# FFN layer two: the fifth outer product by seven inner products, inner weights made from the blocks in SBUF, and a first step emitted with high priority

## The chip, the cores and the metric

The kernel runs on one core of one Trainium2 chip. The metric is the device time of one execution in microseconds (us). The core has five engines with an instruction queue each: PE (TensorE, matmuls, with its weight loads shown apart as PEld), DVE (VectorE), ACT (ScalarE), POOL (GpSimd) and SP (SyncE, which here only issues DMAs). An engine takes its instructions in order, so an instruction that waits holds up all that stand behind it on that engine.

## The reference, cut to what matters

```python
def reference(x, ...):                       # x: 1 x 2048 x 1024, float32
    ...                                      # token mixers, output projection -> h
    hn2 = rmsnorm(h, norm2_g)
    up = jnp.einsum('bsd,df->bsf', hn2, w_up)        # 2048 x 1024 @ 1024 x 4096
    act = jnp.square(jax.nn.relu(up))
    h = h + jnp.einsum('bsf,fd->bsd', act, w_down)   # 2048 x 4096 @ 4096 x 1024
    return rmsnorm(h, final_g)
```

The change concerns the product `act @ w_down`, called layer two here.

## The kernel before

All activations are held transposed, features on the 128 partitions and 512 tokens along the row. A float32 operand of a matmul is split into a high part `hi` (ACT, L146) and a rest `lo` (DVE, L147), and a product is three matmuls: weight hi by row hi, weight hi by row lo, weight lo by row hi. Each matmul is 128x128 by 128x512.

**Outer products.** Both feed-forward layers go by the Winograd form of Strassen's scheme: the weights are four blocks, the tokens two halves (`PAIRS`, two times 512 tokens each), the features two halves, and seven products P1 to P7 of sums of blocks take the place of eight. In layer two (`down`) the row operands are the seven sums A11, A12, A22, S1, S2, S3, S4 of activations, which layer one (`up`) leaves in DRAM as `sd[q][i]`, with q the half of the product's columns. A plain outer product is 8 steps, one for each 256 features (`kk`), and a step is 2 values of q x 4 blocks of 128 output features x 2 chunks of 128 features x 3 matmuls, 48 matmuls, 384 in the eight (L1390).

**Inner products.** P4 and P2 (`SPLIT`) are themselves made by the same scheme, of seven inner products on blocks of a quarter of the size: 28 steps of 12 matmuls, 336 (L1228). They need sums of quarter blocks of the weights (`wi`) and of the rows (`sdi`). The sums of rows are made in `up` as the activations come out (`inner_rows` loads the other half's rows, `inner_sums` makes four sums and stores them, L870 and L879 to L887). The sums of weights are made in `down`, in the steps of the outer product ahead (`inner_weights`, `prepare`): quarter blocks are loaded again from DRAM (L1088, rows of 1 KB), subtracted in place (L1096) and stored (L1097). The order is P1, P6, P7, P4, P5, P2, P3.

**Weights of the outer products.** `make` builds a step's operands: `blk` loads a block of weights of 512 KB (L1121), `minus` makes a difference of two blocks in place (L1125) and can store it as `td[0]` or `td[1]` (L1127) for a later product; two row tiles `ar` are loaded (L1171) and split into `ad`, the weights into `wd`. P1 loads b11, and for `td[0]` also b12; P6 takes `td[0]`, b22 and b21 and leaves `td[1]`; P7 takes b12 and b22; P5 takes `td[0]` again.

**What runs ahead.** `make_ahead` emits operands of steps until six row operands and three weight operands are ahead of the matmuls. The buffers are five of `ar`, six of `wr`/`wq` (loaded weights), three of `wd` and five of `ad`. All these pools of `down` lie in memory that `up` used, so their first tiles wait until `up` has let go of it.

**Results.** `evac` and `inner_step` take the sums in PSUM (tile `pb`, eight banks) into the tiles p1, u2, u3, c21; a POOL-issued DMA adds the residual h to them (`add_residual`); `final` makes the sums of squares for the last norm, on ACT and DVE. P5 as a plain product ends with 16 additions on DVE, onto u3 and u2. The last outer product, P3, runs for one q after the other, with the last norm of finished parts between its steps and the rest behind it.

**What sets the order.** The program is written as a plain sequence; a scheduler then places the instructions of all engines by their dependences and by its own estimates of durations, so the order on each engine isn't that of the text. `tc.high_priority()` puts what is emitted in it ahead of other work that is ready. At the boundary between the layers the operands of the first steps of `down` are therefore loaded and split among the last activations of `up` (`post`, L976 to L1025).

Of the kernel before, what the change touches and what calls it, by code (L numbers as in the profile page):

```python
# [46 lines left out]
def hymba_block(ctx: ExitStack, tc: tile.TileContext, xT, gains, w_in, pool_w, w_out, w_up, w_down, out):  # L47
# [64 lines left out]
    for i in range(PAD):  # L112
# [24 lines left out]
    sdi = {i: [[dram.tile([P, 2, T], F32, name=f"sdi{i}_{n}_{c}") for c in range(4)] for n in range(4)] for i in (1, 2)}  # L137
    wi = {i: {n: [dram.tile([P, 4, 256], F32, name=f"wi{i}_{n}_{c}") for c in range(2)]
              for n in ("P5", "P6", "P7", "P4")} for i in (1, 2)}
    td = [[dram.tile([P, 2, T], F32, name=f"td{i}_{c}") for c in range(8)] for i in range(2)]  # L140
# [717 lines left out]
    def up(pools, more):  # L858
# [110 lines left out]
        def post(q, m, s):  # L969
# [4 lines left out]
            def put(i, t):  # L974
                if q == 0 or m >= NM // 2 or i not in (A12, A22):
                    nc.sync.dma_start(sd[q][i][m // 2][:, m % 2], t)  # L976
                if q and i in (A12, A22):
                    inner_sums(m, i, t)
# [23 lines left out]
            elif s == "P7":  # L1002
                copy("u3")
# [64 lines left out]
    def down(pools):  # L1068
        t8, s8, rs, rt, pupa, pup, rsp, rlp, tmp_, psb = pools

        SPLIT = {"P4": A22, "P2": A12}
        order = (("P1", A11), ("P6", S2), ("P7", S3), ("P4", A22), ("P5", S1), ("P2", A12))
        steps = []
        for n, i in order:
            if n in SPLIT:
                steps += [(n, p, kk, None) for p in ("P1", "P5", "P6", "P3", "P7", "P2", "P4") for kk in range(4)]
            else:
                steps += [(n, i, kk, (0, 1)) for kk in range(8)]
        steps += [("P3", S4, kk, (q,)) for q in range(2) for kk in range(8)]
        made = {}  # L1080

        def quarter(of, kp, x, y):
            t = rt.tile([P, 4, 256], F32, tag="wr", name="wq")
            v = t.rearrange("p (k c) n -> p k c n", k=2)
            for k in range(2):
                at = 2 * kp + k + 4 * x
                src = w_down[of, at] if isinstance(of, int) else td[int(of[1]) - 1][at]
                nc.sync.dma_start(v[:, k], src[:, :, y * 256:(y + 1) * 256])  # L1088
            return t

        def inner_weights(n):

            i, res = SPLIT[n], []

            def less(to, x, y, p, kp):
                nc.vector.tensor_tensor(to, x, y, ALU.subtract)  # L1096
                nc.sync.dma_start(wi[i][p][kp], to)  # L1097

            for kp in range(2):
                b = {}  # L1100

                def take(x, y, b=b, kp=kp):
                    return lambda: b.update({(x, y): quarter(source[n], kp, x, y)}), lambda: None
                op = lambda to, x, y, p, b=b, kp=kp: (lambda: None, lambda: less(b[to], b[x], b[y], p, kp))
                res += [take(0, 0), take(0, 1), op((0, 0), (0, 1), (0, 0), "P5"), take(1, 1),
                        op((0, 1), (1, 1), (0, 1), "P7"), op((1, 1), (1, 1), (0, 0), "P6"), take(1, 0),
                        op((1, 0), (1, 0), (1, 1), "P4")]
            return res

        prep, source = [], {"P4": "t2", "P2": 2}  # L1110

        def prepare(n):

# [460 lines left out]
```

## Time and profile before

| what | value |
|---|---|
| runs: median, lowest to highest of three | 1929.7 us, 1928.63 to 1931.03 us |
| the profiled execution: its own time, its span | 1929.1 us, 1927.3 us |
| busy: DVE, ACT, POOL | 1365.9 us, 990.4 us, 177.3 us |
| layer one, `up` (matmuls L1052) | about 695 to 1308.8 us of the span |
| layer two: P1, P6, P7 | 1313.5 to 1576.9 us |
| P4 (inner) | 1576.9 to 1653.1 us |
| P5 | 1653.1 to 1740.1 us |
| P2 (inner) | 1740.1 to 1816.3 us |
| P3 and the last norm | 1816.3 us to the end |
| DMA traffic | 483.44 MB, mean 251 GB/s |

How to read it: a line of groups has the line of the kernel, the engine, the operation, the tiles written and read, their shapes, the count, then the busy time in us and the mean time of one in ns. Durations of successive instructions on an engine can overlap by some 0.1 us; the distance between starts is the cost in the queue. A stretch of the trace ("windows") gives its length, then for each engine the busy time and the instructions in brackets, then the clock that TensorE was granted (1.00 is full speed), the share of time in which the DMA engines were busy and their rate in GB/s. A list of instructions gives start, duration, engine, line, operation, tiles, count, and in brackets the idle time ahead of it with what ended it.

### The profile page before, as it was taken

The numbers are of one execution on the slowest core, as the hardware profiler recorded it, in microseconds if no ns is written. First come the engines' busy times: TensorE is split into PE (matmuls) and PEld (weight loads), VectorE is DVE, ScalarE is ACT, GpSimd is POOL, SyncE is SP. The second block draws the span as 40 slices with busy tenths as digits, with TensorE's granted clock in tenths as the row PEclk, the third lists the DMA queues.
The fourth block names the chain that finished last, engine by engine and source line by source line (L and its number), as shares of the span: only waits on it lengthen the run. The fifth ranks groups of instructions, "written<-read, shape, count | busy, mean of one in ns | idle before, by whom it ended". The sixth has DMA issues, their size and how long they took to land.

```text
span 1927.3 us, 26270 instructions
## 1 busy us (share of the span) xinstructions
PE 1903.3 (99%) x9043; PEld 1588.9 (82%) x9043; DVE 1365.9 (71%) x2026; ACT 990.4 (51%) x1580; POOL 177.3 (9%) x399
## 2 busy tenths in 40 slices
PE   9999999999999999999999999998999999999997
PEld 7888888888888888888888888887888888888886
DVE  6887799667866976667678767776555547648874
ACT  5565566455554455555576555553333255426643
POOL 0211123101211120000000000000010010002120
PEclk9999999999999999999999999999999999999999
DMA  7685686887797864676667566669798888959852
GB/s 224 206 273 179 222 277 212 262 310 262 263 344 277 304 204 150 211 248 228 212 230 253 195 219 221 243 248 396 268 326 291 276 251 312 333 192 303 312 207 90
DMA packets 197359, 483.44 MB, mean 251 GB/s; under 512 B 22496, under 2 KB 42976, under 8 KB 193120
## 3 DMA queue, kind: packets, MB, share of 16 engines
q1 hardware_dynamic: 192464, 473.01, 70.9%
q0 software_dynamic: 4608, 8.39, 2.4%
q8 instruction: 73, 1.20, 0.3%
q14 instruction: 70, 0.57, 0.1%
q10 hardware_dynamic: 144, 0.26, 0.1%
HBM read 320.10 MB, written 161.48 MB: 250 GB/s over the span
## 4 chain that ended last, share of the span: by engine, by line
PE 92%; DVE 4%; DMA 2%; issue 1%; POOL 1%; ACT 1%; SPq 0%; DVEq 0%; ACTq 0%; POOLq 0%
PE pb L1390 22%; PE pY L1052 17%; PE pZ L1052 9%; PE pb L1228 8%; PE pd L175 8%; PE pd L176 8%; PE pd L177 8%; PE pX L1052 4%; PE po L672 2%; PE pta L661 1%; PE pm L202 1%; PE pz L614 1%; PE pr L228 1%; PE pz L615 1%; PE pb L1333 1%
## 5 line engine op out<-in xcount | busy, mean ns | idle before, releaser
L1390 PE MATMUL pb<-ad,wd 128*128 128x512 f32 x1872 | 429.4, 391 | 4.7 <-ACT ad L146 4.7
L1390 PEld LDWEIGHTS pb<-ad,wd 128*128 128x128 f32 x1872 | 352.3, 189 | 78.1 <-ACT ad L146 5.1
L1052 PE MATMUL pY<-sa,hw 128*128 128x512 f32 x1536 | 364.1, 389 | 0.7 <-ACT u L987 0.7
L1052 PEld LDWEIGHTS pY<-sa,hw 128*128 128x128 f32 x1536 | 288.1, 188 | 60.9 <-ACT u L987 1.1
L175 PE MATMUL pd<-h,hl 128*128 128x512 f32 x752 | 300.0, 399 | 0.7 <-DVE qkr L421 0.7
L176 PE MATMUL pd<-h,hl 128*128 128x512 f32 x752 | 297.4, 395 | 0.0
L177 PE MATMUL pd<-h,hl 128*128 128x512 f32 x752 | 297.2, 395 | 0.0
L146 ACT ACTIVATE ad<-ar 128x1024 fp32r<-128x1024 f32 x136 | 142.4, 1052 | 116.2 <-PE pb L1390 69.9
L147 DVE TENSOR_TENSOR ad<-ar,ad 128x1024 fp32r<-128x1024 f32 x136 | 164.8, 1222 | 39.6 <-ACT ad L146 39.5
L1052 PE MATMUL pZ<-sa,hw 128*128 128x512 f32 x768 | 184.6, 389 | 0.0
L1052 PEld LDWEIGHTS pZ<-sa,hw 128*128 128x128 f32 x768 | 144.1, 188 | 29.9
L175 PEld LDWEIGHTS pd<-h,hl 128*128 128x128 f32 x752 | 142.3, 189 | 28.4 <-DVE qkr L421 1.0
L177 PEld LDWEIGHTS pd<-h,hl 128*128 128x128 f32 x752 | 142.2, 189 | 27.9
L176 PEld LDWEIGHTS pd<-h,hl 128*128 128x128 f32 x752 | 142.1, 189 | 27.1
L146 ACT ACTIVATE hl<-raw 128x512 fp32r<-128x512 f32 x168 | 104.2, 631 | 111.0 <-PE pd L177 67.2
L1228 PE MATMUL pb<-ad,wd 128*128 128x512 f32 x672 | 152.7, 389 | 0.0
L147 DVE TENSOR_TENSOR hl<-raw,hl 128x512 fp32r<-128x512 f32 x168 | 114.3, 687 | 53.6 <-ACT hl L146 50.0
L1228 PEld LDWEIGHTS pb<-ad,wd 128*128 128x128 f32 x672 | 126.1, 188 | 26.2
L146 ACT ACTIVATE wd<-wr 128x1024 fp32r<-128x1024 f32 x48 | 50.9, 1062 | 151.2 <-PE pb L1390 129.5
L147 DVE TENSOR_TENSOR hw<-rt,hw 128x512 fp32r<-128x512 f32 x128 | 87.6, 688 | 57.3 <-ACT hw L146 56.5
L147 DVE TENSOR_TENSOR wd<-wr,wd 128x1024 fp32r<-128x1024 f32 x48 | 58.6, 1223 | 62.0 <-ACT wd L146 62.0
L1052 PE MATMUL pX<-sa,hw 128*128 128x512 f32 x384 | 93.1, 389 | 0.0
(213 smaller groups left out, 2591.6 us busy)
## 6 DMA issues: line engine op xcount, KB each, us to landing
ar<-sd SPq DMA_DIRECT2D x104, 512.0 KB, 5.7
rb<-in_w_up_dram SPq DMA_DIRECT2D x32, 1024.0 KB, 5.8
wr<-in_w_down_dram SPq DMA_DIRECT2D x64, 512.0 KB, 5.5
sd<-a SPq DMA_DIRECT2D x112, 256.0 KB, 3.2
raw<-in_w_in_dram SPq DMA_DIRECT2D x50, 512.0 KB, 4.3
sd<-s SPq DMA_DIRECT2D x96, 256.0 KB, 3.5
raw<-in_w_out_dram SPq DMA_DIRECT2D x32, 512.0 KB, 5.5
ar<-sdi SPq DMA_DIRECT2D x32, 512.0 KB, 7.2
```

The costliest lines, as they stand in the source:

```text
L146: nc.scalar.activation(hi, src, AF.Copy)
L147: return nc.vector.tensor_tensor(lo, src, hi.bitcast(F32), ALU.subtract)
L175: nc.tensor.matmul(ps, hl[:, 0, c], hi, start=(k == 0), stop=False)
L176: nc.tensor.matmul(ps, hl[:, 0, c], lo, start=False, stop=False)
L177: mm = nc.tensor.matmul(ps, hl[:, 1, c], hi, start=False, stop=(k == n - 1))
L202: marks["pm"] = nc.tensor.matmul(pm[:, c:c + 1], ss[:, c * P:(c + 1) * P], inv[n], start=(i == 0), stop=(i == len(parts) - 1))
L228: mm = nc.tensor.matmul(pr[:, b * P:(b + 1) * P], yr[:, x, b:b + 1].to_broadcast([P, P]), identr, start=(b == 0 and x == 0), stop=(b == TB ...
L614: nc.tensor.matmul(pz, qa[:, qsl], k, start=first, stop=False, skip_group_check=not (first and last))
L672: nc.tensor.matmul(po[:, p * 256 + to:p * 256 + to + hi - lo], vw[:, 2 * p + v], at[:, x, lo:hi], start=(p == 0 and n == 0 and x == 0), sk ...
L1052: nc.tensor.matmul(t, w[:, wx, c], a[:, ax, c % 2], start=first and c == 0 and x == 0, stop=last and c == G - 1 and x == 2, skip_group_che ...
L1228: nc.tensor.matmul(b, t[:, wx, 2 * (kk % 2) + c, i * P:(i + 1) * P], a[:, ax, c], start=p in ("P1", "P5", "P2") and kk == 0 and c == 0 and ...
L1390: nc.tensor.matmul(ps[q, n], t[:, wx, c, n * P:(n + 1) * P], left_[q][:, ax, c], start=(n_ in ("P1", "P5", "P3") and kk == 0 and c == 0 an ...
```

## The change

1. **P5 joins P4 and P2.** It is made by seven inner products (`SPLIT` gets P5, with the rows S1). Its 16 additions at the end become 28, four behind each inner product, on u3 and on u2, and the residuals are added as a part is complete.
2. **`up` makes the inner sums of S1** as well as of A12 and A22: for each of the eight pairs of columns with q = 1 two more loads of rows, four more operations on DVE, four more stores, and one store of S1 less.
3. **Inner weights from blocks in SBUF.** `quarter` loads for the sums, `prepare` and its list go. A block's last use in a step is now to be turned into the inner differences in place (`more_weights`, `inner_weights`: four subtractions of 128x512 and four stores of 256 KB for each pair of blocks kk, kk + 4). To have both in SBUF, the steps of P1, P6 and P7 run in the order 0, 4, 1, 5, 2, 6, 3, 7 (`TURN`). P1 makes those of `td[0]` (for P5), P6 those of `td[1]` (for P4), P7 loads b12 once more and makes those for P2. The order inside a weight block is changed on the host, so that a half of its columns lies in one piece (`half`, `block`).
4. **P6's b21 gets a buffer of its own**, `rtx`, one tile. Half of `td[1]` is stored for kk below 4.
5. **The first step of P1 is emitted with high priority**, without its differences, which follow (`late`).

The diff, cut:

```diff
-    sdi = {i: [[dram.tile([P, 2, T], F32, name=f"sdi{i}_{n}_{c}") for c in range(4)] for n in range(4)] for i in (1, 2)}
+    sdi = {i: [[dram.tile([P, 2, T], F32, name=f"sdi{i}_{n}_{c}") for c in range(4)] for n in range(4)] for i in (1, 2, 3)}
...
             def put(i, t):
-                if q == 0 or m >= NM // 2 or i not in (A12, A22):
+                if q == 0 or m >= NM // 2 or i not in (A12, A22, S1):
                     nc.sync.dma_start(sd[q][i][m // 2][:, m % 2], t)
-                if q and i in (A12, A22):
+                if q and i in (A12, A22, S1):
                     inner_sums(m, i, t)
...
             elif s == "P7":
+                if q and m >= NM // 2:
+                    inner_rows(m - NM // 2, S1)
                 copy("u3")
...
-        SPLIT = {"P4": A22, "P2": A12}
+        SPLIT = {"P4": A22, "P5": S1, "P2": A12}
+        TURN = (0, 4, 1, 5, 2, 6, 3, 7)
...
-                steps += [(n, i, kk, (0, 1)) for kk in range(8)]
+                steps += [(n, i, kk, (0, 1)) for kk in TURN]
...
+        def inner_weights(i, kk, t):
+            if kk < 4:
+                tops[i] = t
+                return
+            b, k = {(x, y): half(w, y) for x, w in enumerate((tops.pop(i), t)) for y in range(2)}, kk - 4
+            for to, x, y, p in (((0, 0), (0, 1), (0, 0), "P5"), ((0, 1), (1, 1), (0, 1), "P7"),
+                                ((1, 1), (1, 1), (0, 0), "P6"), ((1, 0), (1, 0), (1, 1), "P4")):
+                nc.vector.tensor_tensor(b[to], b[x], b[y], ALU.subtract)
+                nc.sync.dma_start(wi[i][p][k // 2][:, 2 * (k % 2):2 * (k % 2) + 2], b[to])
...
+        def more_weights(n, kk, w):
+            if n == "P1":
+                minus(blk(1, kk), w)
+                nc.sync.dma_start(td[0][kk], w)
+                inner_weights(S1, kk, w)
+            elif n == "P6":
+                minus(blk(2, kk, rtx), w)
+                if kk < 4:
+                    nc.sync.dma_start(half(td[1][kk], 0), half(w, 0))
+                else:
+                    nc.sync.dma_start(td[1][kk], w)
+                inner_weights(A22, kk, w)
+            elif n == "P7":
+                inner_weights(A12, kk, blk(2, kk))
...
+            late.append(lambda: more_weights(n, kk, w))
+            if g:
+                late.pop()()
...
-            elif n_ == "P5":
-                add(val("u3", q), val("u3", q))
-                add_residual(val("u3", q)[:, n], j1, 1, n)
-                add(val("u2", q), val("u2", q))
-                add_residual(val("u2", q)[:, n], j0, 1, n)
...
+                    for name in {"P4": ("c21",), "P5": ("u3", "u2"), "P2": ("p1",)}[n_]:
+                        to = val(name, q)[:, n]
+                        nc.vector.tensor_tensor(to, b, to, ALU.add)
...
+                        elif n_ == "P5":
+                            add_residual(to, PAIRS[q][name == "u3"], 1, n)
...
+        with tc.high_priority():
+            make_ahead(1)
+        late.pop()()
         make_ahead()
         for g, (n_, i, kk, qs_) in enumerate(steps):
-            if n_ in ("P7", "P5") and kk == 0:
-                prep.extend(inner_weights("P4" if n_ == "P7" else "P2"))
-                prep[0][0](), prep[1][0]()
-            if n_ in ("P7", "P5"):
-                prepare(2)
```

The scheduler places other rows too. Three places show it, all at the boundary between the layers, where the last activations of `up` and the first operands of `down` share DVE and ACT. L881 to L887 are the inner sums of rows; L1012 to L1021 before, L1014 to L1023 now, are the last sums and the last activation of `up` (the row that reads `pZ` is the one behind the very last matmuls of `up`); L1125 before and L1115 now is `minus`; L1106 is a subtraction of `inner_weights`.

DVE before, from the third weight operand of `down` to the first row operands:

```order
L147 TENSOR_TENSOR wd<-wr,wd 128x1024
L881 TENSOR_TENSOR j_13261<-a_13105,a_13256 128x512
L1125 TENSOR_TENSOR wr<-wr 128x1024
L883 TENSOR_TENSOR j_13262<-j_13261,hr 128x512
L885 TENSOR_TENSOR hr<-hr,a_13105 128x512
L887 TENSOR_TENSOR hr<-hr,j_13262 128x512
L1012 TENSOR_TENSOR s_13286<-a_13283,a_13256 128x512
L1015 TENSOR_TENSOR s_13289<-s_13286,a_13204 128x512
L1017 TENSOR_TENSOR a_13283<-a_13204,a_13283 128x512
L1021 TENSOR_TENSOR a_13306<-pZ,u_13224 128x512
L147 TENSOR_TENSOR ad<-ar,ad 128x1024 x5
```

Between the third `minus` and the row that reads `pZ` stand six rows, and the row operands `ad` follow that row.

DVE now, from the same place, first part:

```order
L147 TENSOR_TENSOR wd<-wr,wd 128x1024
L881 TENSOR_TENSOR j_13379<-a_13220,a_13374 128x512
L1115 TENSOR_TENSOR wr<-wr 128x1024
L883 TENSOR_TENSOR j_13380<-j_13379,hr 128x512
L885 TENSOR_TENSOR hr<-hr,a_13220 128x512
L887 TENSOR_TENSOR hr<-hr,j_13380 128x512
L1106 TENSOR_TENSOR wr<-wr 128x512 x4
```

and on to the first row operands:

```order
L1014 TENSOR_TENSOR s_13404<-a_13401,a_13374 128x512
L881 TENSOR_TENSOR j_13407<-s_13269,s_13404 128x512
L1019 TENSOR_TENSOR a_13401<-a_13318,a_13401 128x512
L1106 TENSOR_TENSOR wr<-wr 128x512
L883 TENSOR_TENSOR j_13408<-j_13407,hr 128x512
L1017 TENSOR_TENSOR s_13417<-s_13404,a_13318 128x512
L885 TENSOR_TENSOR hr<-hr,s_13269 128x512
L887 TENSOR_TENSOR hr<-hr,j_13408 128x512
L1023 TENSOR_TENSOR a_13434<-pZ,u_13338 128x512
L147 TENSOR_TENSOR ad<-ar,ad 128x1024 x5
```

The four subtractions of `inner_weights` and a fifth one, and the four inner sums of S1, now stand between `minus` and the row that reads `pZ`: fifteen instructions where there were six. The first `ad` still follows that row.

ACT before, the last activations of `up` and the first rows of `down` (L981 and L982 are relu and square):

```order
L981 ACTIVATE a_13204<-a_13204 128x512
L982 ACTIVATE a_13204<-a_13204 128x512
L987 ACTIVATE u_13254<-pY 128x512
L146 ACTIVATE wd<-wr 128x1024
L981 ACTIVATE a_13256<-a_13256 128x512
L982 ACTIVATE a_13256<-a_13256 128x512
L981 ACTIVATE a_13283<-pY 128x512
L982 ACTIVATE a_13283<-a_13283 128x512
L981 ACTIVATE a_13306<-a_13306 128x512
L146 ACTIVATE ad<-ar 128x1024 x5
```

and ACT now:

```order
L987 ACTIVATE u_13372<-pY 128x512
L981 ACTIVATE a_13318<-a_13318 128x512
L982 ACTIVATE a_13318<-a_13318 128x512
L146 ACTIVATE wd<-wr 128x1024
L981 ACTIVATE a_13374<-a_13374 128x512
L982 ACTIVATE a_13374<-a_13374 128x512
L981 ACTIVATE a_13401<-pY 128x512
L982 ACTIVATE a_13401<-a_13401 128x512
L146 ACTIVATE ad<-ar 128x1024 x2
L981 ACTIVATE a_13434<-a_13434 128x512
L146 ACTIVATE ad<-ar 128x1024 x3
```

The first two row operands `ad` have moved ahead of the relu on the last activation; the rest still follows it. Before, a pair L981, L982 on an earlier activation stood ahead of the copy L987, and the third weight operand `wd` followed the copy directly; now that pair stands between the copy and the weight operand.

101 lines of the change are left out of this document (39 added, 62 removed).

## The prediction

> **What bounds the kernel now.** I read the page first, then the waits of PE, then the chain of work that ended last.
>
> ```profile
> span 1927.3 us, 26270 instructions
> PE 1903.3 (99%) x9043; PEld 1588.9 (82%) x9043; DVE 1365.9 (71%) x2026; ACT 990.4 (51%) x1580; POOL 177.3 (9%) x399
> ```
> ```profile
> PE pb L1390 <- ACT ad L146: 4.7, 1, 4.7
> PE pzero L327 <- DVE zero L95: 1.5, 1, 1.5
> ```
> ```profile
> 1313.51 263.43 PE pb L1390 x1152
> 1576.94 76.16 PE pb L1228 x336
> 1653.10 87.04 PE pb L1390 x384
> 1740.14 76.17 PE pb L1228 x336
> ```
>
> PE is busy for all but 24 us of the span. It waits for operands once for long: 4.7 us, at the boundary between the layers. Inside layer two it runs without a stop: 336 matmuls take 76.16 us and 384 take 87.04 us, 226.7 ns each in both forms. So a change pays here if it takes matmuls away or closes that gap, and costs where it makes PE wait.
>
> The gap has a tail. These stretches run across it; the last but two column is the granted clock:
>
> ```profile
> 1308.00:1310.00 2.00, 0.82 (x4) 0.36 (x2) 1.94 (x4) 0.43 (x1) 0.00 (x0) 1.00 1.06 414
> 1310.00:1313.50 3.50, 0.00 (x0) 0.00 (x0) 1.86 (x4) 1.62 (x3) 0.00 (x0) 0.65 1.01 412
> 1313.50:1316.00 2.50, 2.49 (x6) 2.01 (x7) 2.50 (x3) 2.50 (x3) 0.00 (x0) 0.50 1.06 419
> 1316.00:1318.00 2.00, 2.00 (x7) 1.55 (x6) 2.00 (x2) 1.77 (x3) 0.00 (x0) 0.53 1.01 405
> 1318.00:1320.00 2.00, 2.00 (x11) 1.64 (x10) 1.97 (x4) 0.00 (x0) 0.00 (x0) 1.00 1.05 405
> ```
>
> In the gap the clock falls, stays at half until about 1318, and PE then does 13 matmuls in 4.5 us. The 1152 matmuls take 263.43 us where 1152 x 0.2267 is 261.1: this tail costs 2.3 us. The boundary costs 7.0 us in all.
>
> **The change part by part.** *P5.* 384 matmuls become 336: 87.04 - 76.16 = 10.9 us off PE. This is the one gain that needs nothing else.
>
> *The boundary.* What holds PE there is DVE. These are its rows from the trace, the third weight operand to the first rows of `down`:
>
> ```profile
> 1304.38 1.23 DVE L147 TENSOR_TENSOR wd<-wr,wd 128x1024 fp32r<-128x1024 f32 x1 [0.34 <-ACT wd L146]
> 1305.56 0.69 DVE L881 TENSOR_TENSOR j<-a,a 128x512 f32<-128x512 f32 x1
> 1306.17 1.22 DVE L1125 TENSOR_TENSOR wr<-wr 128x1024 f32<-128x1024 f32 x1
> 1307.30 0.68 DVE L883 TENSOR_TENSOR j<-j,hr 128x512 f32<-128x512 f32 x1
> ...
> 1311.16 0.69 DVE L1021 TENSOR_TENSOR a<-pZ,u 128x512 f32<-128x512 f32 x1
> 1313.49 5.77 DVE L147 TENSOR_TENSOR ad<-ar,ad 128x1024 fp32r<-128x1024 f32 x5 [1.64 <-ACT ad L146]
> ```
> ```profile
> 1305.94 2.88 PE L1052 MATMUL pZ<-sa,hw 128*128 128x512 f32 x12
> 1302.44 0.60 ACT L987 ACTIVATE u<-pY 128x512 f32<-128x512 f32 x1 [1.53 <-PE pY L1052]
> 1303.28 1.07 ACT L146 ACTIVATE wd<-wr 128x1024 fp32r<-128x1024 f32 x1 [0.24 <-DMA wr<-in_w_down_dram]
> 1304.24 0.62 ACT L981 ACTIVATE a<-a 128x512 f32<-128x512 f32 x1
> 1304.89 0.63 ACT L982 ACTIVATE a<-a 128x512 f32<-128x512 f32 x1
> 1307.80 0.64 ACT L982 ACTIVATE a<-a 128x512 f32<-128x512 f32 x1
> ```
>
> PE ends `up` at 1305.94 + 2.88 = 1308.8. The row L1021, which reads its last result, starts only at 1311.16: from 1306.17 on DVE runs without idling, a `minus`, six rows of 128x512 at a distance of 0.64 us (3.86 / 6), then L1021. It is late, not waiting. The order above shows nine more rows of that size in this place: five subtractions of inner weights and four inner sums of S1. DVE pays 9 x 0.64 = 5.8 us more before it is through with the row that reads `pZ`. That row releases the second row operand on ACT, and behind it on DVE stand all `lo` parts of the rows. The high priority has moved the first `hi` part ahead, so PE can do the four products hi by hi of q = 0 early, 0.9 us, and then waits on.
>
> In numbers: `minus` is also later, since L981 and L982 on an earlier activation now stand between the copy L987 and the weight operand on ACT, 2 x 0.65 less the 0.24 idle, so it starts at about 1307.3. Then 1.13 + 15 x 0.64 + 0.69 ends the `pZ` row at 1318.8; the second `hi` takes 1.1 us more on ACT; PE goes on at 1319.9. Idle: 1319.9 - 1308.8 - 0.9 = 10.2 us, for 4.7 before, + 5.5 us. The half clock behind it stays, 2.3 us in both.
>
> The subtractions work in place, so they also wait until the block's store has landed:
>
> ```profile
> wr<-in_w_down_dram SPq DMA_DIRECT2D x11, 512.0 KB, 8.1
> td<-wr SPq DMA_DIRECT2D x3, 512.0 KB, 6.8
> ```
>
> A store takes 6.8 us around the boundary. That of the third `minus` is issued at about 1308.5 and lands at 1315.3; by its own queue DVE reaches the subtraction behind it at 1308.4 + 10 x 0.64 = 1314.8. So + 0.5 us: the boundary costs 6.0 us more than before. Its ends: 4.4 us if neither the ACT order nor a store delays anything, 10 us if stores land as late as the slowest 11.1 us load there, `wr` in this row of the chain:
>
> ```profile
> 1292.18 11.07 DMA wr<-in_w_down_dram
> ```
>
> The Trainium skill, "DMA: Bandwidth & Descriptors", section "Anatomy of one DMA", fits a DMA by 2.0 us and bytes at 436 GB/s, which is an estimate of 3.2 us for 512 KB. By that no store would be in the way and the sum would be 0.5 us lower; the measured 6.8 us speaks against it here, where the queue is full.
>
> *More sums in `up`.* 32 more operations on DVE, 32 x 0.64 = 20.5 us, and 10.5 MB more traffic (8 pairs of columns x 5 x 256 KB) in this stretch:
>
> ```profile
> 1005.00:1309.00 304.00, 303.14 (x1337) 250.35 (x1335) 226.00 (x352) 170.81 (x297) 0.00 (x0) 1.00 0.66 235
> 1309.00:1402.00 93.00, 88.49 (x381) 73.10 (x382) 50.42 (x48) 32.05 (x36) 5.44 (x6) 0.96 0.88 319
> 1402.00:1490.00 88.00, 88.00 (x390) 72.86 (x389) 45.71 (x40) 29.13 (x34) 1.74 (x2) 1.00 0.93 317
> 1653.00:1740.00 87.00, 87.00 (x386) 72.03 (x385) 44.79 (x45) 25.71 (x26) 6.44 (x8) 1.00 0.75 252
> 1740.00:1816.00 76.00, 76.00 (x337) 62.91 (x336) 66.82 (x73) 48.62 (x55) 7.60 (x9) 1.00 1.02 331
> ```
>
> DVE goes from 226 to some 247 of 304 us and DMA from 0.66 to some 0.75: hidden by PE's 303. I take 0; without that cover it would be 2.6 us for each of the eight pairs.
>
> *P1 and P6 (rows two and three).* Counted from the program in blocks of 512 KB, P1 moved 40 (two weights, two rows and a store in each of eight steps), and the stores of inner weights make it 48; P6 moved 48, now 54. Shares of 0.88 and 0.93 become about 1.05 in both, 4 to 5 us too much in each stage. DVE gets 16 subtractions in each, 10 us, and waits for stores, and in P6 for the one buffer of b21. The cover is the lead of the operands:
>
> ```profile
> 1338.71 1.23 DVE L147 TENSOR_TENSOR wd<-wr,wd 128x1024 fp32r<-128x1024 f32 x1 [4.21 <-ACT wd L146]
> ```
> ```profile
> DVE wr L1125 <- DMA wr<-in_w_down_dram: 31.3, 7, 6.4
> ```
>
> This weight operand is made as the second step ends (1313.51 + 2.3 + 2 x 10.88 = 1337.6) and needed two steps of 10.9 us later, at 1359.3: 19 us of lead. In P6 DVE already waits 31.3 us for weights, up to 6.4 us at once, and PE never stops. I take 0 and keep + 13 us as the other end (third rival).
>
> *P5's own work.* DVE has 42 splits of 1.15 us (5.77 / 5) and 28 additions of 0.64, 66 us of 76; P2's stage has 66.82 of 76 (row five) without a stop. The residuals fall in its second half instead of at its end. I take 0; the other end is the second rival.
>
> *Sum.* - 10.9 + 6.0 = - 4.9 us, 1924.2 us by the profiled execution's own 1929.1. The median of the runs shown lies 0.6 us above that, so **1924.8 us**.
>
> **The rivals.** *First: the gap closes.* If the first step runs as the priority asks, PE stops for some 0.7 us (ACT is through with the last L982 at 1308.4, the split takes 1.05), and neither the 4.7 us nor the 2.3 us are paid: 1929.7 - 10.9 - 6.3 = 1912.5 us. ACT's order speaks for it, DVE's fifteen rows ahead of the first `lo` against it. By the Trainium skill, "TensorE: Matmul & The Clock Gate", section "What's actually happening", the clock halves after about 3.4 us of idling; the rows agree with that (4.7 us, then 0.50), and a gap of 0.7 us would keep it whole.
>
> *Second: P5 waits for its own sums.* ACT squares u3 for the last norm as soon as its residuals have landed, ahead of splits for P2:
>
> ```profile
> ACT sq L1247 <- DMA u<-hs: 9.6, 4, 4.3
> u<-hs POOLq DMA_DIRECT2D x9, 256.0 KB, 14.2
> ```
>
> The longest of these waits was 4.3 us and hidden. Residuals now follow the inner products one by one, and inner steps have a lead of four steps of 2.7 us, 10.9. If a 14.2 us landing isn't covered, some 5 us are lost: 1929.8 us.
>
> *Third, the other side: P6 runs DVE late.* A pair of steps has 6 splits, 4 `minus` and 4 subtractions, 6.9 + 4.5 + 2.6 = 14.0 us, of 21.8. Two waits of 4 us for stores and two of 2.5 us for b21, both inside the 6.4 us of the row above, make it 27, 5.2 us too long, 21 us over the four pairs. It decides as soon as this is more than the lead that is left. With the 19 us whole it costs next to nothing; if the late start at the boundary and P1's full DMA leave 8 us, PE loses 13: 1938 us. For it: shares above 1, in-place work behind stores. Against it: P6's 42 us in which DVE is idle now.
>
> **How the numbers follow.** Forecast 0.62, its own range 1923 to 1929 by the boundary's two ends; first rival 0.09, second 0.12, third 0.17. A measurement here can tell about 0.2% from no change, so faster is below 1925.8 and slower above 1933.6. The forecast falls below 1925.8 as long as the boundary costs under 7.0 us more, some three quarters of its chance: 0.47; with the first rival 0.56. The rest of the forecast and most of the second rival make no change, 0.26; the third, and a little of the second, make slower, 0.18. The range that leaves out the first rival and most of the third is 1916 to 1934 us.
>
> **What would show it.** Right: 336 matmuls in 76.2 us for P5; PE idle for 9 to 11 us at the boundary in two pieces with four matmuls between them, the longer one ending with the first rows' split, half clock behind it; no wait of PE in P1, P6 and P7; DMA shares near 1 in P1 and P6. Wrong: a boundary of under 3 us (first rival), waits of PE for `wd` or `ad` in P6 (third) or at the start of P2 (second), or stops in the second half of `up`, where I counted nothing.

## The result and the profile after

| | median, lowest to highest | runs |
|---|---|---|
| before | 1929.56 us, 1927.54 to 1933.19 | 7 |
| changed | 1937.83 us, 1933.86 to 1939.64 | 7 |

The ratio is 1.0043, with a 95% interval of 1.0033 to 1.0053: the change makes the kernel 8.3 us slower, where 4.9 us faster were forecast, and the time lies outside the forecast's range of 1916 to 1934 us. The profiled execution took 1938.5 us.

The head of the page, then all waits of PE above 1.7 us:

```profile
span 1936.7 us, 26464 instructions
PE 1895.5 (98%) x8995; PEld 1581.6 (82%) x8995; DVE 1425.2 (74%) x2120; ACT 1008.5 (52%) x1598; POOL 177.2 (9%) x399
```
```profile
PE pb L1392 <- ACT ad L146: 16.2, 2, 9.8
PE pY L1054 <- ACT u L987: 4.4, 2, 3.1
PE pm L202 <- DVE ss L186: 2.7, 1, 2.7
```

The span is 9.4 us longer. PE works 7.8 us less than before and waits more: 16.2 us for the first row operands, where it was 4.7. The chain of work that ended last (start, us, what) says where the ground is lost:

```profile
1297.82 7.91 DMA wr<-in_w_down_dram
1305.75 8.89 DMA wr<-in_w_down_dram
1315.94 7.62 DMA td<-wr
1333.58 263.10 PE pb L1392 x1148
1596.68 168.65 PE pb L1221 x744
1771.16 54.47 PE pb L1221 x239
1825.64 5.45 PE pb L1392 x24
```

P7 ends at 1596.7, before at 1576.9: 19.7 us later. The three inner products end at 1825.6, 229.0 us behind it, where P4, P5 and P2 took 239.4: 10.4 us regained. And the chain ahead of P1 is now made of DMAs, two weight loads and the store of a difference. PE's rows across the boundary (start, us, operation, count, and in brackets the idle time ahead):

```profile
1301.39 2.88 PE L1054 MATMUL pY<-sa,hw 128*128 128x512 f32 x12
1307.35 4.62 PE L1054 MATMUL pY<-sa,hw 128*128 128x512 f32 x12 [3.08 <-ACT u L987]
1312.33 3.02 PE L1054 MATMUL pZ<-sa,hw 128*128 128x512 f32 x12 [0.36 <-DVE a L1007]
1321.69 2.07 PE L1392 MATMUL pb<-ad,wd 128*128 128x512 f32 x4 [6.34 <-ACT ad L146]
1333.58 11.72 PE L1392 MATMUL pb<-ad,wd 128*128 128x512 f32 x39 [9.82 <-ACT ad L146]
```
```profile
1300.00:1310.00 10.00, 6.92 (x27) 5.35 (x26) 5.23 (x6) 4.27 (x7) 0.00 (x0) 0.92 1.04 392
1310.00:1320.00 10.00, 4.99 (x17) 3.21 (x16) 6.63 (x9) 2.89 (x4) 0.00 (x0) 0.84 1.04 410
1320.00:1330.00 10.00, 2.07 (x4) 1.16 (x4) 5.87 (x10) 1.60 (x3) 0.00 (x0) 0.50 1.03 412
```

PE stops four times, 3.08 + 0.36 + 6.34 + 9.82 = 19.6 us, against 0.7 + 4.7 = 5.4 before. Its clock falls more than once: 12 matmuls in 4.62 us (2.72 at full speed, 12 x 0.2267), four in 2.07 (0.91), 1148 in 263.10 (260.2), in all with the `pZ` row 6.2 us for 2.3 before. (A row of matmuls with a stop behind it shows some 0.16 us more than that product, 2.88 for twelve, so a little of the 6.2 is the stops themselves.) 14.2 + 3.9 = 18.1 us are lost here; 1.3 us more are a wait for a load in the middle of `up` (below), and the rest is the start of `up`, 0.3 us later.

The second fence has the surprise. In these 30 us DVE, whose fifteen rows were to be the bound, is busy for 5.23 + 6.63 + 5.87 = 17.7 us, ACT for 8.8. The DMA engines are full (shares of 1.03 and 1.04). The DMA waits of DVE and ACT from 1285 to 1335 (us in total, times, longest):

```profile
DVE wr L1115 <- DMA wr<-in_w_down_dram: 3.4, 3, 1.6
DVE wr L1106 <- DMA td<-wr: 2.4, 1, 2.4
DVE j L883 <- DMA sd<-s: 2.0, 1, 2.0
DVE s L1014 <- DMA sdi<-j: 1.1, 1, 1.1
DVE a L1007 <- DMA sd<-s: 0.7, 1, 0.7
ACT wd L146 <- DMA wr<-in_w_down_dram: 10.3, 3, 4.2
```

Before, DVE waited for no DMA there, and ACT 0.2 us for a weight load. But ACT had one wait for a store already, just ahead of a row that the prediction shows:

```profile
1307.17 0.60 ACT L981 ACTIVATE a<-pY 128x512 f32<-128x512 f32 x1 [1.64 <-DMA sd<-s]
```

Three kinds of wait stand here now. Weight loads are late (`wr`): they take no longer than before (median 8.2 us, before 9.6), but SP issues them later, five from 1290.6 to 1302.5 us where six went out from 1288.4 to 1294.8. The subtractions wait for the store of the difference (`td`). And rows that write a fresh tile, L883, L1014, L1007, wait for a *store* of another (`sd`, `sdi`): they need a tile of the pool `av`, and its last content hasn't been stored yet. All are waits in order: L1007 takes a result out of PSUM, and PE waits for that; every row of `up` behind a wait waits too. On ACT the same activation as above now waits 5.83 us for its tile, which DVE frees with L885:

```profile
1319.43 0.60 ACT L981 ACTIVATE a<-pY 128x512 f32<-128x512 f32 x1 [5.83 <-DVE hr L885]
```

The first split of rows stands behind it on ACT, so PE's stop of 6.34 us ends there.

### The profile page after: what moved, and what is told of

Same layout as the page of the kernel before. It is cut to its first block, busy times and chain, and to the rows that moved or that the text cites. A ratio compares the mean times of both kernels' runs of the same rounds, so it can differ in the third digit from the quotient of the medians.

```text
span 1936.7 us, 26464 instructions
## 1 busy us (share of the span) xinstructions
PE 1895.5 (98%) x8995; PEld 1581.6 (82%) x8995; DVE 1425.2 (74%) x2120; ACT 1008.5 (52%) x1598; POOL 177.2 (9%) x399
## 4 chain that ended last, share of the span: by engine, by line
PE 92%; DVE 3%; DMA 3%; issue 1%; ACT 1%; POOL 0%; SPq 0%; DVEq 0%; ACTq 0%; POOLq 0%
PE pb L1392 17%; PE pY L1054 17%; PE pb L1221 12%; PE pd L175 8%; PE pd L176 8%; PE pd L177 8%; PE pZ L1054 8%; PE pX L1054 4%; PE po L672 2%; PE pta L661 1%; DMA wr<-in_w_down_dram 1%; PE pm L202 1%; PE pz L614 1%; PE pz L615 1%; PE pr L228 1%
## 5 line engine op out<-in xcount | busy, mean ns | idle before, releaser
L1392 PE MATMUL pb<-ad,wd 128*128 128x512 f32 x1488 | 343.9, 393 | 16.2 <-ACT ad L146 16.2
L1392 PEld LDWEIGHTS pb<-ad,wd 128*128 128x128 f32 x1488 | 281.1, 189 | 75.5 <-ACT ad L146 17.3
L1221 PE MATMUL pb<-ad,wd 128*128 128x512 f32 x1008 | 228.9, 389 | 0.2 <-DVE ad L147 0.2
L1221 PEld LDWEIGHTS pb<-ad,wd 128*128 128x128 f32 x1008 | 189.2, 188 | 39.8 <-DVE ad L147 0.6
L146 ACT ACTIVATE ad<-ar 128x1024 fp32r<-128x1024 f32 x148 | 155.5, 1052 | 117.4 <-PE pb L1392 49.4
L147 DVE TENSOR_TENSOR ad<-ar,ad 128x1024 fp32r<-128x1024 f32 x148 | 179.6, 1221 | 43.5 <-ACT ad L146 43.5
L146 ACT ACTIVATE wd<-wr 128x1024 fp32r<-128x1024 f32 x40 | 42.4, 1061 | 130.0 <-PE pb L1392 106.1
L146 ACT ACTIVATE hw<-rt 128x512 fp32r<-128x512 f32 x128 | 80.0, 626 | 28.0 <-PE pZ L1054 19.5
```

Of the source, the lines that this page charges most:

```text
L146: nc.scalar.activation(hi, src, AF.Copy)
L147: return nc.vector.tensor_tensor(lo, src, hi.bitcast(F32), ALU.subtract)
L1221: nc.tensor.matmul(b, t[:, wx, 2 * (kk % 2) + c, i * P:(i + 1) * P], a[:, ax, c], start=p in ("P1", "P5", "P2") and kk == 0 and c == 0 and ...
L1392: nc.tensor.matmul(ps[q, n], block(t, wx, c, n), left_[q][:, ax, c], start=(n_ in ("P1", "P3") and kk == 0 and c == 0 and x == 0), stop=(n ...
```

## The experiments

Five of the kernels compute other numbers in part: where S1's sums are left out or hollow (no sums; DMAs alone and operations alone, both with and without late subtractions), P5's rows are other rows of the same size. All else keeps all of the work. Each run was timed beside the kernel before on its chip; the last column is the difference of the medians. By the intervals a row is uncertain by 2 to 4 us, and the difference of two rows by some 3 to 5.

| kernel | median us | ratio, 95% interval | us to before |
|---|---|---|---|
| changed | 1937.8 | 1.0043, 1.0033 to 1.0053 | + 8.3 |
| without the priority | 1935.7 | 1.0033, 1.0021 to 1.0046 | + 6.4 |
| before, with the priority | 1927.4 | 0.999, 0.998 to 1.0 | - 1.9 |
| late subtractions | 1930.0 | 1.0003, 0.9994 to 1.0013 | + 0.7 |
| no sums of S1 | 1915.8 | 0.9932, 0.9916 to 0.9949 | - 13.5 |
| S1's DMAs alone | 1929.2 | 0.9995, 0.9986 to 1.0005 | - 1.0 |
| S1's operations alone | 1934.3 | 1.002, 1.001 to 1.003 | + 4.1 |
| S1's DMAs alone, late subtractions | 1920.8 | 0.995, 0.9933 to 0.9966 | - 8.4 |
| S1's operations alone, late subtractions | 1925.7 | 0.9974, 0.9962 to 0.9987 | - 3.5 |
| first weights loaded by POOL | 1936.3 | 1.0033, 1.0023 to 1.0042 | + 7.1 |
| last pair's sums in P7 | 1926.5 | 0.9978, 0.9968 to 0.9988 | - 3.7 |
| the same, late subtractions | 1922.6 | 0.996, 0.9946 to 0.9974 | - 7.6 |
| the same, first weights by POOL | 1923.5 | 0.9968, 0.9956 to 0.9979 | - 5.8 |
| sums in place | 1931.5 | 1.0011, 1.0001 to 1.0021 | + 2.0 |
| sums in place, late subtractions | 1923.0 | 0.9959, 0.9944 to 0.9973 | - 6.6 |
| sums in place, late subtractions, last pair in P7 | 1918.6 | 0.9929, 0.9906 to 0.9952 | - 11.0 |
| before, with the priority, 11 tiles | 1935.2 | 1.0025, 1.0015 to 1.0036 | + 5.6 |

**Is it the priority?**

```diff
-        with tc.high_priority():
-            make_ahead(1)
+        make_ahead(1)
```

> The changed kernel without the high priority on the first step; all else as changed. In its order the first rows' splits on ACT go back behind the relu of the last activation, and one copy of PSUM stands ahead of the first weight operand; the first two copies of the last columns still stand next to weight operands that wait for loads, and DVE's order at the boundary is the same but for one row. Theory A (subtractions of inner weights, in place behind stores, ahead of the row that reads pZ): no difference, within 2 us of the changed kernel's 1937.8, so 1936 to 1940 us; PE's long wait before its 9th matmul of P1 stays near 10 us. Theory B (the inner sums of S1 fill DVE and the DMA slots of the last columns): the same. Theory C (the priority itself: the splits of weights wait on ACT for loads ahead of copies that PE needs): the 3.1 us wait of PE for a copy and its half clock go, 1932 to 1934 us.

> The kernel before with the high priority on the first step alone. Theory C: it is slower by 3 to 5 us, 1933 to 1935 us, since splits of weights that wait for loads stand ahead of copies on ACT as in the changed kernel. Theories A and B: the priority does little by itself; the first rows' splits come some 3 us earlier on ACT but the pZ row and the low parts on DVE stand where they stood: 1926 to 1930 us.

The changed kernel without it is 1.9 us better, the kernel before with it also 1.9 us. So it isn't the cause; what it costs or gives, about 2 us, is no more than the uncertainty. In the changed kernel without it PE's wait for the first rows didn't stay near 10 us: it was one of 17.7. In the kernel before it splits the one stop of 4.7 us into two shorter ones, and the 1148 matmuls behind them take 261.9 us (260.2 at full speed):

```profile
PE pb L1392 <- ACT ad L146: 3.0, 2, 2.4
```
```profile
1314.16 261.88 PE pb L1392 x1148
```

**Are the subtractions in the way?** In `make`, the splits of `ad` are collected, and `more_weights` of the first three steps is emitted behind the fourth:

```diff
-            if g:
+            if g > 2:
                 late.pop()()
...
-        late.pop()()
         make_ahead()
+        with tc.issue_after(behind_[3].ins):
+            while late:
+                late.pop(0)()
```

> The changed kernel, but the differences and inner weights of the first three steps of P1 are queued on DVE behind the low parts of the first four row operands. Nothing is left out. Theory A: three minus of 1.14 us, five subtractions of 0.64 us and their waits for loads and stores (1.4 + 1.6 + 0.4 + 2.4 us in the trace) leave the way of the row that reads pZ: 12 us, and with a shorter gap 1 to 2 us of half clock, 1924 to 1927 us. Theory B: the loads of weights stay late, since the sums of S1 are still there: 1932 to 1936 us. Theory C: PE's 3.1 us wait for a copy stays, the rest too: 1935 to 1938 us.

7.6 us; 1930.0 us lies between the two ranges expected. The same edit was worth 7.4 us where S1 had only its DMAs, 7.6 us where it had only its operations, and 8.6 us with the sums in place. In a fifth pair, where the last sums of S1 are made later (below), it was worth 3.9 us only; its price seems to depend on what else stands at the boundary. And it isn't the price of the subtractions alone: `more_weights` moves the three `minus` with them, which stood ahead of the `pZ` row in the kernel before too. No run moves the subtractions by themselves.

**Are the sums of S1 in the way?**

> The changed kernel without the inner sums of S1 in the first layer: P5 reads the sums of A22 in their place, so P5 is computed from wrong rows at the same cost, and the rows of S1 are all stored as before. In its order the subtractions of inner weights also stand behind the pZ row, so this takes away what theories A and B name together. A and B together: the boundary as before the change, 7 us, and P5's 10.9 us gained: 1918 to 1920 us. If it is no better than the kernel with the late inner weights alone, B adds nothing; the difference between the two is B's share. Theory C: PE's wait for a copy behind a weight operand stays, 1935 us.

22 us below the changed kernel, and below the 1918 to 1920 us expected. But without these sums the scheduler itself put the subtractions behind the `pZ` row, so this run has both causes taken away; against late subtractions, the sums cost 0.7 + 13.5 = 14.2 us. (The `minus` rows differ here: they stand ahead of the `pZ` row without the sums, behind it in the kernel with late subtractions. If that placing is worth something, the sums cost so much more and the subtractions so much less.) PE then stops for 3.1 us for the first rows:

```profile
PE pb L1390 <- ACT ad L146: 3.1, 2, 2.3
```

**Their DMAs, or their operations?** One kernel stores the four tiles without the operations; the other replaces the loads by a POOL memset and leaves the stores out.

```diff
+            if i == S1:
+                for n, v in enumerate((a, t, r[0], r[1])):
+                    keep(n, v)
+                return
```
```diff
-            keep = lambda n, v: nc.sync.dma_start(sdi[i][n][m // 2][:, m % 2], v)
+            keep = lambda n, v: None if i == S1 else nc.sync.dma_start(sdi[i][n][m // 2][:, m % 2], v)
```

> The changed kernel with S1's loads and stores in `up` kept, and its four operations on DVE left out (the stored tiles aren't the sums, so P5's rows are other numbers at the same cost). Leaving out S1's inner sums altogether gave 1915.8 us. Theory B1 (what costs is S1's DMAs: with two loads and four stores a pair of columns in the queue, the first weights and rows of `down` land later, and DVE and ACT wait in order for them): at least two thirds of the difference stays, 1928 to 1936 us, PE's waits at the boundary 12 us or more, half clock behind them. Theory B2 (what costs is the four operations on DVE, 2.6 us a pair, and their place ahead of the `pZ` row): 1915 to 1922 us, PE's waits under 6 us.

> The other half: S1's four operations on DVE kept, its loads replaced by a POOL memset of the same tile and its stores left out (P5 takes A22's stored sums, so its rows are other numbers at the same cost). B1 (DMAs): 1915 to 1921 us, the weights and rows of `down` landing as in the kernel before, PE's waits at the boundary 3 to 6 us. B2 (DVE): 1928 to 1936 us, with waits of 12 us or more. If both halves come out between 1921 and 1928, the two add up and neither is the cause alone.

Each half came out in the range of the theory that makes it the cause, so neither theory held alone. In both the subtractions stood ahead of the `pZ` row again, so both were run with late subtractions:

> S1's loads and stores without its four operations on DVE (as two runs before; P5's rows are other numbers at the same cost), and the subtractions of the first three steps queued behind the first four row operands on DVE. The run with the DMAs alone had 1929.2 us, the one without S1's sums 1915.8 us, but there the scheduler had put the subtractions behind the `pZ` row by itself; this pair differs from it in the DMAs alone. If the subtractions (A, 8 us) and S1's DMAs are costs that add up: 1919 to 1923 us. If the DMAs cost nothing once the subtractions are out of the way: 1914 to 1918 us. If the DMAs are the whole of the 14 us between 1915.8 and the 1930.0 us of the kernel with late subtractions: 1927 to 1931 us.

> S1's four operations on DVE without its loads and stores (a POOL memset in place of the loads; P5 takes A22's stored sums), and the subtractions of the first three steps queued behind the first four row operands. Costs that add up: the 1934.3 us of the run with the operations alone less 8 us, 1924 to 1928 us. If DVE's operations cost nothing once the subtractions are out of the way: 1914 to 1918 us. For both halves together the sums over 1915.8 us should make the 14 us of the kernel with late subtractions, if nothing but these two is at work.

Over the kernel without the sums (- 13.5) the DMAs cost 5.1 us, the operations 10.0, together 15.1 for the 14.2 of the whole: they add up within the uncertainty. But 10 us is four times what a pair's operations last (2.6 us), so they bring more than DVE time. (The memsets on POOL aren't it: DVE waits for none of them, and its rows last 0.69 us as before.) In the run with the operations alone and late subtractions, which has no store of S1's tiles, DVE waits for stores of others:

```profile
1302.96 0.69 DVE L1000 TENSOR_TENSOR a<-pX,p 128x512 f32<-128x512 f32 x1 [0.80 <-DMA sdi<-hr]
1310.87 0.69 DVE L1010 TENSOR_TENSOR a<-pZ,u 128x512 f32<-128x512 f32 x1 [2.27 <-DMA sd<-s]
1314.61 0.69 DVE L886 TENSOR_TENSOR j<-j,hr 128x512 f32<-128x512 f32 x1 [0.99 <-DMA sd<-s]
1317.76 0.69 DVE L1017 TENSOR_TENSOR s<-a,a 128x512 f32<-128x512 f32 x1 [1.14 <-DMA sdi<-j]
```

L1010 is late by 2.27 us, and PE waits 4.33 us for it. The pool `av` has 13 tiles; the inner sums of a pair of columns take 12 of them now and took 8, so it comes round sooner to a tile whose store is still under way. The late weights, too, go with the operations and not with the DMAs: ACT waited 7.2 us for weight loads in the run with S1's operations alone, and 0.7 us in the one with its DMAs alone.

**Are the loads late because of SP's order?** The third weight block was issued at 1297.8, behind a store for which SP itself had waited 1.2 us, until another store (`sdi<-j`) had landed. Issued by POOL instead, which is idle there:

```diff
-            nc.sync.dma_start(t, w_down[i, kk] if isinstance(i, int) else td[int(i[1]) - 1][kk])
+            (nc.gpsimd if first and kk in TURN[:3] else nc.sync).dma_start(...)
```

> The changed kernel with all of its work, but the six weight loads of the first three steps (b11 and b12 of kk = 0, 4, 1) are issued by POOL, which has nothing else to do there, and not by SP, where they stand between S1's loads and stores. Theory L (the loads are late because SP takes its rows in order and each store of a sum waits there for DVE): the six loads are issued within some 7 us of each other from the time the buffers are free, PE's waits at the boundary fall by 3 to 10 us, 1927 to 1934 us. If they are late because the DMA engines are full, they land no sooner and the time stays within 2 us of the changed kernel's 1937 us.

No gain. Weights come earlier, ACT waits for none; but a store of a sum took 12.62 us (the median of the eight of its kind there was 6.8), and `up` waits for its tile. That it was late because the loads beside it took their share of full DMA engines is our reading, not tested:

```profile
1295.25 12.62 DMA sdi<-hr
```
```profile
1307.90 0.69 DVE L997 TENSOR_TENSOR a<-pX,p 128x512 f32<-128x512 f32 x1 [6.54 <-DMA sdi<-hr]
```
```profile
1315.17 5.05 PE L1054 MATMUL pZ<-sa,hw 128*128 128x512 f32 x12 [8.17 <-DVE a L1007]
```

**Is it the last columns alone?** The last pair's rows of S1 are stored, and its sums made in the first step of P7 (`last_sums`: four loads, four operations, four stores).

> The changed kernel, all of its work kept, but the inner sums of S1 for the last of the eight pairs of columns are made in `down` during the first step of P7 (four loads, four operations, four stores there) and not at the end of `up`. If the cost of S1's sums is paid at the boundary alone (B, in either form), the time falls by some 8 to 14 us against the changed kernel, to 1922 to 1929 us, and PE's waits at the boundary to under 10 us; `up`'s other seven pairs cost nothing. If it is spread over the last columns (a queue that has been filled earlier), it falls by under 4 us. The in-place subtractions still stand ahead of the `pZ` row (theory A), so the time stays above 1919 us.

> The run before with the subtractions of the first three steps queued behind the first four row operands on DVE as well. If A (subtractions ahead of the `pZ` row, about 8 us) and B (S1's sums at the boundary) are separate costs that add up: 1914 to 1919 us, both waits of PE together under 5 us, faster than the kernel before by 0.5 to 0.8%. If they are one cost, paid once by whichever is last: no more than 2 us below the run before.

12.0 us from one pair of eight, 8.3 us with late subtractions; P7 and what follows pay nothing for it. The second run missed its 1914 to 1919 us, and it isn't the other case either: the late subtractions gave 3.9 us, neither 8 nor 2 at most. The two costs seem to overlap in part. A shortage was left, DVE waiting 2.77 us ahead of the last `pZ` row itself:

```profile
1316.40 0.69 DVE L1026 TENSOR_TENSOR a<-pZ,u 128x512 f32<-128x512 f32 x1 [2.77 <-DMA sd<-s]
```

With the first weights by POOL as well it was no better, 1923.5 us:

> The three remedies at once, all of the work kept: S1's last sums made in P7, the subtractions of the first three steps behind the first row operands, the first six weight loads issued by POOL. Without the last of them it was 1922.6 us with 8.7 us of waits of PE around the boundary, where ACT waited up to 3.8 us for a weight block. By theory L: 1913 to 1919 us and waits under 5 us. If the loads aren't late through SP: 1921 to 1925 us.

**Is it the tiles?** One tile less for each inner sum of rows, at the same operations and DMAs:

```diff
-            s1, s2 = (avp.tile([P, T], F32, tag="av", name=n) for n in ("j1", "j2"))
-            nc.vector.tensor_tensor(s1, a, t, ALU.add)
-            keep(0, s1)
-            nc.vector.tensor_tensor(s2, s1, r[0], ALU.subtract)
-            keep(1, s2)
+            s2 = avp.tile([P, T], F32, tag="av", name="j2")
             nc.vector.tensor_tensor(r[0], r[0], a, ALU.subtract)
             keep(2, r[0])
+            nc.vector.tensor_tensor(s2, t, r[0], ALU.subtract)
+            keep(1, s2)
+            nc.vector.tensor_tensor(a, a, t, ALU.add)
+            keep(0, a)
```

> The changed kernel with the same operations, loads and stores, but `inner_sums` takes three tiles of the pool `av` and not four: r0 - a first, then t - r0, then a + t in place of a, so that j1 falls away (9 tiles for a pair of columns, where the changed kernel takes 12 and the kernel before 8). Theory M (what the inner sums of S1 cost beside their DMAs is tiles: a tile of `av` comes free only when its store has landed, 7 to 12 us later where the queue is full, and with 13 tiles the last activations of `up` wait for one on DVE, with all that stands behind them): 1927 to 1933 us. If it is DVE's time for the four operations: within 2 us of the changed kernel's 1937 us.

> The run before, and the subtractions of the first three steps queued behind the first four row operands on DVE. All of the work is kept. With four tiles it was 1930.0 us. M: 1919 to 1925 us, that is the 1915.8 us without S1's sums, 5 us for its DMAs, and no more than a third of the 10 us for its operations; no wait of DVE for `sd` or `sdi` stores above 1 us before the `pZ` row. DVE's time: 1928 to 1932 us.

6.3 us, and 7.3 us with late subtractions: what was left of the operations' 10.0 us is 6.9 - 5.1 = 1.8 us, within the uncertainty. The same four operations are still done, so DVE's time for them was at most a small part of the price. One part of the expectation missed: a wait for a tile above 1 us is still there.

```profile
1309.21 0.69 DVE L1007 TENSOR_TENSOR a<-pZ,u 128x512 f32<-128x512 f32 x1 [4.16 <-DMA sd<-s]
```

Then the tiles by themselves: the kernel before with the priority, and `spool("avp", 11)` for 13.

> The kernel before with the first step at high priority (1927.4 us) and 11 tiles in the pool `av` in place of 13: no operation and no DMA more. M: the tile alone has a price, 3 to 8 us, 1930 to 1936 us, with waits of DVE or ACT for `sd` or `sdi` stores ahead of the `pZ` row. If tiles are not what is short: 1926 to 1929 us.

Two tiles fewer and nothing added cost 5.6 + 1.9 = 7.5 us. The third weight operand, too, moved by a place in DVE's order; the wait itself is this:

```profile
1317.51 0.69 DVE L1015 TENSOR_TENSOR s<-s,a 128x512 f32<-128x512 f32 x1 [5.20 <-DMA sd<-a]
```
```profile
PE pb L1392 <- ACT ad L146: 8.9, 2, 7.4
```

**All remedies but POOL.**

> Sums in place, late subtractions, and the last pair's S1 sums made in P7: all of the work kept. With four tiles it was 1922.6 us. M: 1915 to 1920 us, since the waits of 2.8 and 1.6 us for `sd` stores at the boundary go. If the last pair was all of the shortage: 1921 to 1924 us.

1918.6 us, all of the work kept: 11.0 us faster than the kernel before, and 19 below the changed one. PE's waits for row operands are down to 2.7 us, and DVE waits for no DMA from 1300 to 1328; ACT still waits 2.3 us for a store (`sd<-s`):

```profile
PE pb L1410 <- ACT ad L146: 2.7, 2, 1.6
```

## Why the prediction was wrong

The account of the runs: P5 - 10.9, priority - 1.9, S1's sums + 14.2, subtractions (with `minus`) + 7.6, in all + 9.0 us; measured + 8.3. The last two are steps from one run to the next, so with the - 13.5 us of the kernel without sums they make + 8.3 by construction; what the account tests is that - 10.9 - 1.9 = - 12.8 is near - 13.5. By the fifth pair the split between the two also depends on the order in which they are taken away. By the prediction's own steps:

- *P5, - 10.9 us: right.* These are the stages of P4, P5 and P2 in the changed kernel:

```profile
1597.00:1673.00 76.00, 76.00 (x337) 62.96 (x336) 59.61 (x59) 45.72 (x49) 1.68 (x2) 1.00 0.91 300
1673.00:1749.00 76.00, 76.00 (x337) 62.96 (x336) 64.47 (x70) 42.92 (x43) 10.66 (x12) 1.00 0.95 298
1749.00:1826.00 77.00, 76.82 (x339) 63.29 (x339) 66.06 (x71) 49.67 (x56) 3.54 (x4) 1.00 0.97 337
```

- *The boundary, + 6.0 us with ends of 4.4 and 10: the step that failed.* It was + 18.1 us. "DVE pays 9 x 0.64 = 5.8 us more": the nine rows were costed by their duration, with every input and every tile there when DVE came to them. The kernel before allowed that reading on DVE, which ran without idling; ACT's wait of 1.64 us for a store was the sign against it. These are the third `minus` and the `pZ` row now:

```profile
1314.73 1.23 DVE L1115 TENSOR_TENSOR wr<-wr 128x1024 f32<-128x1024 f32 x1 [0.40 <-DMA wr<-in_w_down_dram]
1331.76 0.69 DVE L1023 TENSOR_TENSOR a<-pZ,u 128x512 f32<-128x512 f32 x1
```

The forecast had the `minus` start at 1307.3 and the `pZ` row end at 1318.8. The `minus` is 7.4 us late, behind late weights (ACT waited 10.3 us for three of them) and a wait for a tile. From there to the end of the `pZ` row it takes 6.2 us more than forecast, and 6.0 of them are waits between the fifteen rows: 1.96 and 1.10 for tiles being stored, 2.39 for the store of the difference, 0.55 between two rows of DVE. The rows themselves lasted what they were costed at.

What the nine rows brought with them was missing from the sum: four more tiles a pair of columns, drawn from a pool of 13 whose stores land 6 to 8 us after their issue there. Of the sums' 14.2 us the last pair's operations lasted 2.6. That the tiles have such a price is shown by the sums in place (6.3 and 7.3 us) and by the pool of 11 (7.5 us). Why SP issued the weights later was not found; they were late without S1's DMAs, and issuing them earlier gained nothing.

For the five subtractions the sum had 5 x 0.64 + 0.5 = 3.7 us; the edit that moves them gave 7.6, but moves the `minus` rows too. Their wait for the store was seen, at 0.5 us; it was 2.39. Even the upper end, 10 us, held only one mechanism, a store of the difference. The sign for being right, two pieces with four matmuls between them, came true in form, with 6.34 + 9.82 = 16.2 us for the 9 to 11.
- *The half clock, "2.3 us in both": wrong.* More stops gave more slow stretches, 6.2 us.
- *More sums in `up`, 0: right* up to the last columns. One wait of 1.3 us at 1004.8, for the first split of rows loaded for the second half, stands in each traced kernel whose first step has the priority (1.2 to 1.9 us), and not in the two without it; in the changed kernel that load lands 7.6 us after its issue, before 6.0. Why it does was not tried.
- *P1 and P6, 0: right.* From 1340 to 1830 the only wait of PE is 0.2 us. So the third rival, 1938 us, had the time by luck: its place, P6, was wrong. DMA shares were 0.92 in P1, hardly more than the 0.88 before, and 1.01 in P6, for a forecast of about 1.05 in both:

```profile
1345.00:1427.00 82.00, 82.00 (x364) 67.91 (x363) 47.24 (x46) 27.86 (x31) 7.18 (x8) 1.00 0.92 313
1427.00:1515.00 88.00, 88.00 (x390) 72.90 (x389) 60.56 (x62) 28.94 (x32) 0.00 (x0) 1.00 1.01 363
```

- *P5's own work, 0: right*, and the second rival fell: P2 starts without a wait.
- *First rival, 1912.5 us:* the kernel without S1's sums comes nearest, 1915.8 us, with stops of 0.80 and 2.34 us and half clock behind the second. Beyond P5's 10.9 it gains 2.6 of the rival's 6.3 us.

What stays open: the price of S1's DMAs alone (5.1 us) contains two more tiles a pair for the loaded rows, and was not split further. No run that keeps the sums has the subtractions behind the `pZ` row and the `minus` rows ahead of it, and none gives the pool more than 13 tiles, the plainest test if tiles are short. Edits of this kind move rows in the scheduler's order too, so each price holds with the order that came with it.

## What to carry to other kernels

Where work is added to an engine that takes its instructions in order, count what each instruction waits for, a load, a store, a fresh tile, and not only how long it lasts; one late tile holds up all behind it; here the operations cost four times their own duration. Set the tiles that a unit of work draws against the size of the pool and the time a store takes to land *in that stretch*: sums in place, three tiles fewer a pair of columns, were worth 6 to 7 us, and two tiles fewer in the pool cost 7.5. At a boundary between stages, queue by hand what is not needed soon (subtractions, last sums) behind the first operands of the next stage; an earlier load was worth nothing here, with DMA shares above 1.

## What had not been expected of the hardware

Over its whole execution the changed kernel's 256 KB stores of `sdi<-hr` land 4.6 us after their issue (median), and 6.9 us from 1285 to 1335. In the kernel whose first weights POOL issues, one took 12.62 us there (its row is above). The Trainium skill, "DMA: Bandwidth & Descriptors", section "Anatomy of one DMA", gives 2.0 us and the bytes at 436 GB/s, an estimate of 2.6 us for 256 KB and 3.2 us for 512 KB; its fit is for DMAs that GpSimd issues, and these stores, like the one for which the prediction used it, are issued by SP. The shortest store of a sum at the boundary, 2.5 us, was near it, most took more than twice that, and the five 512 KB loads that POOL did issue there took 11.2 us (median). The measurement decides.

And the clock fell after a stop of 3.08 us already: the 12 matmuls behind it took 4.62 us for the 2.88 of such a row at full speed. In the kernel without S1's sums two stops of 0.80 and 2.34 us, 3.6 us apart by their matmuls' starts, were enough: the granted clock of the 5 us across the second was 0.66.

```profile
1310.00:1315.00 5.00, 3.43 (x9) 2.76 (x10) 5.00 (x7) 4.54 (x6) 0.00 (x0) 0.66 1.03 412
```

The page "TensorE: Matmul & The Clock Gate" of the Trainium skill, section "What's actually happening", has the clock halve after an idle window of about 3.4 us. The prediction took a gap of 0.7 us as safe by it. By itself such a gap was: behind the 0.80 us stop here the granted clock from 1305 to 1310 was still 1.00. But the stops of 2.34 and 3.08 us, shorter than that window, had half clock behind them.
